# Hybrid decoder block on one core: u for z's last chunk read into idle places of the gates' tile, and two of the first merge's gates read into its first two's place

## The chip, the core and the metric

The kernel runs on one core of one Trainium2 chip. That core has a matrix engine (TensorE, PE in the profile; PEld is its load of weights), a vector engine (VectorE, DVE), a scalar engine (ScalarE, ACT), a general engine (GpSimd, POOL) and an engine that mostly issues transfers (SyncE, SP; its queue is SPq in the profile). Transfers between the device's memory and the core's on-chip memory run on 16 DMA engines beside them. Each engine works through its own list of instructions in order, and semaphores hold an instruction until what it needs is there.

The metric is the time of one execution on the device, in microseconds (us). The median of the timed runs counts.

## The reference

The input is 2048 tokens of 1024 channels. One decoder block is computed; the part that matters here is the mixer and its merge:

```python
h = _rmsnorm(x, norm_pre_mix[layer])
proj = jnp.einsum('bsd,de->bse', h, w_in[layer])
...
u = jax.nn.gelu(proj[..., U0:Z0])
z = jax.nn.gelu(proj[..., Z0:GA0])
gate_a = jax.nn.sigmoid(proj[..., GA0:GB0])
gate_b = jax.nn.sigmoid(proj[..., GB0:IN_WIDTH])
y_attn = _mixer_dilated_attention(q, k, v)
y_gmlp = _mixer_chunked_gmlp(u, z, ln_v_gain[layer], ln_v_bias[layer],
                             w_spatial[layer], b_spatial[layer])
merged = (gate_a * jnp.einsum('bse,ed->bsd', y_attn, w_branch_attn[layer])
          + gate_b * jnp.einsum('bse,ed->bsd', y_gmlp, w_branch_gmlp[layer]))
y = jnp.einsum('bsd,de->bse', merged, w_out[layer])
x = x + _rmsnorm(y, norm_post_mix[layer])
```

`_mixer_chunked_gmlp` normalises z, multiplies it per group of 128 channels with a 128 x 128 matrix over the tokens of a piece, adds a bias, and multiplies the result with u. A squared-ReLU MLP with norms of its own follows.

## The kernel before

All matrix products keep the accuracy of float32 by splitting each operand into a high and a low half (`split`: the high half by ACT or POOL at lines 70 and 72, the low half by DVE or POOL at line 78) and by three matmuls for each product (lines 95 to 97, or the inner loop before line 714). The tokens are worked on in four chunks of 512.

The program has these stages: norm and the products for q, k, v, u and z; the attention, with the product of the gates beside it; the merge and the product with w_out, chunk by chunk; and the MLP. The order of PE's instructions is written by hand. On the other engines a scheduler orders them by when it supposes that they become ready, so an edit at one place can move instructions of ACT, DVE, POOL and SP at others.

**Chunk 3 of z.** `z_chunk` makes four pieces of z for a chunk and leaves the rest of the chunk's work for `sz_out`. That function goes through the four groups g. For each it multiplies on PE (line 554), scales and adds the bias on DVE (line 561, into a tile `sb`), reads u for this group from memory (line 558, into a tile `ur`), multiplies (line 564, on DVE for chunk 3 and in place in `sb`) and stores the product (line 565). `sb` and `ur` have two buffers each for the chunks 2 and 3. For chunk 3, `sz_out` is called from `gates`.

**Gates.** `gates` is the last part of the input's product: the two gates and the first part of u, by a scheme of seven products (`PHASES`) in place of eight. PE's line is 714. Its weights come in pieces (`piece`, line 631: tiles `gr` and `ga`, each split on ACT, DVE or POOL to `spots`). Sums and copies of the products lie in the tiles `gx`, `gz` and `ga` (lines 733 and 735 are the copies by ACT). `gz` holds eight places of 512 columns, `zs[0]` to `zs[7]`; of these the first are filled first, and the later ones lie idle at the start. Results go to memory (line 728). Beside the products of the gates runs the attention's work, unit by unit: scores (lines 894 and 895), a maximum on DVE (lines 908 and 912), exponentials on ACT (line 918), a transpose and the product with v.

**The first merge.** `merge(c, ...)` is called for the chunks 2, 3, 0 and 1 in this order. It goes through eight column tiles dt. For each it fills two banks on PE: `b0` from attention with 6 matmuls, and `b1` from the gMLP with 12. It multiplies each with its gate on DVE (line 1196, for which ACT has put the gate through a sigmoid, line 1179), adds the two (line 1198) and splits the sum to the tile `mg` (ACT line 70, DVE line 78). A gate's name is (chunk, dt, branch); below it is (dt, branch), (5,0) for the first branch's gate of dt 5. A bank comes free for a later dt when DVE has read it.

The first merge (chunk 2) starts with gates read by `early_gates`: the gates of dt 0 to 2 lie in the three tiles `gates0` to `gates2`, which stand in the places of later tiles (`xr`, `gpost`, `gmlp`), and the next ones in a pool of three buffers for branch 0 and two for branch 1 (`load_gate`, line 1170). From dt 3 on the loop loads the gates (dt + 2, 1) and (dt + 3, 0). Beside this merge `spatial_out` does the rest of the gMLP for the chunks 0 and 1 (`sz_out` again) and splits the weights of w_out (`split_wo`: loads `woraw` on POOL's queue at line 1135, halves `wo`). Then `out_block` computes the product with w_out for 128 tokens at a time: it reads the input `xr` (line 1220), which lies in the place of `gates0` and so must wait until that tile is free, and uses it at line 1244. The weights of norms `gpost` and `gmlp` follow to the places of `gates1` and `gates2`. The loads of the next merge's `yt` (line 91) and gates follow on SP.

Of the kernel before, what the change touches and what calls it, by code (L numbers as in the profile page):

```python
# [8 lines left out]
F32 = mybir.dt.float32  # L9
# [7 lines left out]
P = 128  # L17
S = 2048
D = 1024
# [22 lines left out]
def block_kernel(ctx, tc, a, out):  # L42
    nc = tc.nc
    pe, act, dve, pool, sp = nc.tensor, nc.scalar, nc.vector, nc.gpsimd, nc.sync
# [95 lines left out]
    u_d = dtile([4, P, S], "ud")  # L140
    gate_d = dtile([16, P, S], "gated")
    att_d = [dtile([S, 264], f"att{g}") for g in range(3)]
    ya_d = dtile([2, P, S], "yad")
    yg_d = dtile([4, P, S], "ygd")
# [216 lines left out]
    with ExitStack() as e1a:  # L361
# [118 lines left out]
        for half in range(2):  # L480
# [19 lines left out]
            for n, (g, which) in enumerate(qk):  # L500
                w = nxt
# [44 lines left out]

    sgu = {}

    def sz_out(zp, zt, c):
        wsp, bsp, lngb = sgu[c // 2]  # L550
        for g in range(4):
            p = psum_aux(f"sz_{c}{g}")
            for i in range(4):
                pe.matmul(p[:, i * P:(i + 1) * P], zt[:, i, g * P:(g + 1) * P], wsp[:, g, :],
                          start=True, stop=True)
            t = zp.tile([P, 512], F32, name=f"sb_{c}{g}", tag="sz", bufs=2 if c > 1 else 5)
            ut = zp.tile([P, 512], F32, name=f"ur_{c}{g}", tag="ur", bufs=2 if c > 1 else 4)
            sp.dma_start(ut, u_d[g, :, c * 512:(c + 1) * 512])
            bb = bsp[:, g, :]
            bb = bass.AP(tensor=bb.tensor, offset=bb.offset, ap=[list(bb.ap[0]), [0, 4], [1, P]])  # L560
            dve.scalar_tensor_tensor(t.rearrange("p (c i) -> p c i", i=P),
                                     p.rearrange("p (c i) -> p c i", i=P), lngb[:, 0, g:g + 1], bb,
                                     op0=OP.mult, op1=OP.add)
            (dve if c == 3 or c < 2 and g % 2 else pool).tensor_mul(t, t, ut)
            sp.dma_start(yg_d[g, :, c * 512:(c + 1) * 512], t)

    def z_chunk(zp, ws, c):
        zt = zp.tile([P, 4, 512], F32, name=f"z_{c}", tag="z", bufs=2)
# [19 lines left out]
    loaded, late, zps = {}, [], {}  # L588
# [77 lines left out]
    def gates():  # L666
# [2 lines left out]
        slots = [None, hp.tile([P, 2, 2, 4, 512], F32R, name="opB", tag="hT", bufs=2)]  # L669
        zs = wp.tile([P, 8, 512], F32, name="gz", tag="w", bufs=3)  # L670
        zs = [zs[:, n] for n in range(8)]
        xs = [st.tile([P, 512], F32, name=f"gx{n}", tag="ev", bufs=3) for n in range(3)]
        g_["b"].update({(1, 1): hT[2][:, :, :4], (1, 2): hT[2][:, :, 4:]})
        phases = [(half, ops) for half in (1, 0) for ops in PHASES]
        starts, t = {}, 0
# [3 lines left out]
        for t, (half, i, n) in enumerate(seq):  # L679
# [16 lines left out]
            elif todo and (t - t0) % 3 == 1 and t > t0 + 1:  # L696
                w, k = todo.pop(0)
# [13 lines left out]
            p, w, h = bank[n], g_["w"].pop(t), g_["b"][half, i]  # L711
            for k in range(4):
                for m, (l, r) in enumerate(((0, 0), (0, 1), (1, 0))):
                    pe.matmul(p, w[:, l, k], h[:, r, k], start=i in (1, 6, 5, 4) and not k and not m,  # L714
                              stop=k == 3 and m == 2, skip_group_check=True)
                if (t, k) == (3, 2) and late:
                    sz_out(*late.pop(0))
                yield
            if t == 3:
                a = [ga.tile([P, 512], F32, name=f"ga{n_}", tag=f"ga{n_}", bufs=1) for n_ in range(12)]  # L720
# [35 lines left out]
            if i in (2, 5, 3, 4):  # L756
                c, dst = 2 * half + o[2], gate_d if n < 8 else u_d
# [391 lines left out]
    gates = {}  # L1149
# [15 lines left out]
    def load_gate(c, dt, wch):  # L1165
        if dt < KT and (c, dt, wch) not in gates:
            d = chunks.index(c) * KT + dt
            pl, tag = (gtp, f"gt{wch}") if c == 2 or d % (5 - 2 * wch) < 3 - wch else (gxp[0], f"gx{wch}")
            gt = pl.tile([P, 512], F32, name=f"g{wch}_{c}{dt}", tag=tag, bufs=3 - wch if pl is gtp else 2 - wch)
            sp.dma_start(gt, gate_d[wch * 8 + dt, :, c * 512:(c + 1) * 512])  # L1170
            gates[c, dt, wch] = gt
# [10 lines left out]
    def merge(c, yt, between, each=None):  # L1182
        cs = slice(c * 512, (c + 1) * 512)
        mg = []
        for dt in range(KT):
            dsl = slice(dt * P, (dt + 1) * P)
            if dt % 4 == 0:
                mg.append(mgp[dt // 4].tile([P, 2, 4, 512], F32R, name=f"mg{c}{dt}", tag="mg"))
            parts = []
            for wch, ks in ((0, range(0, 2)), (1, range(2, 6))):  # L1190
                open_gate(c, dt, wch)
                gt = gates.pop((c, dt, wch))
                p = psum_mm(f"b{wch}_{c}{dt}")
                for k in ks:
                    mm3(p, wb[k][:, 0, dsl], wb[k][:, 1, dsl], yt[k][:, 0, :], yt[k][:, 1, :], k == ks[0], k == ks[-1])
                dve.tensor_mul(gt, gt, p)
                parts.append(gt)
            dve.tensor_add(parts[0], parts[0], parts[1])
            split(mg[-1][:, 0, dt % 4, :], mg[-1][:, 1, dt % 4, :], parts[0])
            if c != 2:  # L1200
                load_gate(c, dt + 5, 0)
                load_gate(c, dt + 3, 1)
            elif dt > 2:
                load_gate(c, dt + 2, 1)
                load_gate(c, dt + 3, 0)
            if dt < KT - 1:
                for wch in range(2):
                    open_gate(c, dt + 1, wch)
            if each:
                each(dt)  # L1210
            if dt in between:
                between[dt]()
        return mg
# [879 lines left out]
```

## Time and profile before

| what | us |
|---|---|
| timed runs, median of 3 | 2657.37 |
| timed runs, lowest and highest | 2655.06 and 2658.37 |
| the profiled execution's own time | 2654.54 |
| span of the profiled execution | 2652.4 |
| PE busy | 2619.2 |
| DVE busy | 1662.9 |
| POOL busy | 1209.3 |
| ACT busy | 1093.2 |

The mean clock that was granted to PE in the profiled execution is 0.995 of full speed.

A profile's rows are read so. A row of a timeline gives the start of an instruction in the span, its duration (or that of a group of equal ones in a row, with their number behind x), the engine, the line of the program, the operation, the tile it writes and the tiles it reads; in brackets stands for how long the engine was idle ahead of it and what it then waited for. A matmul's row is longer than its share of PE's time, since the next one starts before it ends: matmuls of 512 columns start some 0.23 us apart at full clock, though each row has 0.39. A row "A <- B: total, times, longest" of the view of waits sums the idle time of an engine by what ended it. A row of the view of windows starts with a stretch of time and its length and then has each engine's busy time, PE's granted clock, the share of the DMA engines' time and the GB/s moved.

### The profile page before, as it was taken

The page shows a single profiled execution, that of the slowest core. Times are in us where ns is not written, and L with a number is a line of the kernel's source. Part 1 is how long each engine was busy: PE and PEld are TensorE (multiplying, and loading weights), DVE is VectorE, ACT ScalarE, POOL GpSimd, SP SyncE. Part 2 cuts the span into 40 slices and gives each one's busy share as a digit, 9 for nine tenths or more (in the row PEclk, how much of TensorE's full clock was granted, in tenths as well). Part 3 has the DMA queues.
Part 4 walks back from the last instruction along what each step waited for, and adds up shares of the span by engine and source line. Part 5 has one row for each costly group of instructions (what it writes and reads, how often), then busy time and mean ns, then how long its engine had stood idle before and what let it go on. Part 6 is the DMA issues. An engine that isn't in the chain of part 4 may idle for free. (4 is left out here: it accounts for less than half of the span.)

```text
span 2652.4 us, 35505 instructions
## 1 busy us (share of the span) xinstructions
PE 2619.2 (99%) x12458; PEld 2186.1 (82%) x12458; DVE 1662.9 (63%) x2795; ACT 1093.2 (41%) x2285; POOL 1209.3 (46%) x1093
## 2 busy tenths in 40 slices
PE   9999999999999999899999999999999999999998
PEld 8888888888888878688888888888888888888886
DVE  5676565534533456855677654655437888888866
ACT  5213211244455444444446555655545333323334
POOL 0363354365455555311324473233215677676645
PEclk9999999999999999899999999999999999999999
DMA  8779778888888888744656565644343221222235
GB/s 313 284 249 324 258 232 285 290 281 260 284 296 237 241 289 285 261 149 156 218 192 253 152 222 152 223 132 123 117 145 108 88 77 67 88 88 88 88 114 212
DMA packets 388996, 525.15 MB, mean 198 GB/s; under 512 B 56977, under 2 KB 242065, under 8 KB 387794
## 3 DMA queue, kind: packets, MB, share of 16 engines
q1 hardware_dynamic: 300048, 432.88, 49.7%
q0 software_dynamic: 14992, 51.65, 5.1%
q10 hardware_dynamic: 73778, 38.35, 4.8%
q8 instruction: 98, 1.61, 0.2%
q14 instruction: 80, 0.66, 0.1%
HBM read 339.62 MB, written 183.17 MB: 197 GB/s over the span
## 5 line engine op out<-in xcount | busy, mean ns | idle before, releaser
L1944 PE MATMUL ya<-T_spots,s 128*128 128x512 f32 x1176 | 289.2, 389 | 0.7 <-ACT T_spots L70 0.5
L70 ACT ACTIVATE s<-sraw 128x768 fp32r<-128x768 f32 (+1 forms) x184 | 127.2, 696 | 330.3 <-POOL sraw L1745 155.7
L1944 PEld LDWEIGHTS ya<-T_spots,s 128*128 128x128 f32 x1176 | 220.5, 188 | 47.4 <-ACT T_spots L70 0.9
L78 DVE TENSOR_TENSOR s<-sraw,s 128x512 fp32r<-128x512 f32 x172 | 184.2, 1095 | 8.5 <-ACT s L70 7.2
L1415 PE MATMUL aa<-B,A 128*128 128x512 f32 x768 | 182.3, 390 | 0.7 <-DVE A L85 0.7
L1386 POOL TENSOR_TENSOR s<-w1r 128x512 f32<-128x512 f32 x32 | 42.3, 1321 | 306.6 <-DVE S L78 250.4
L714 PE MATMUL g<-opA,spots 128*128 128x512 f32 x672 | 170.5, 398 | 1.9 <-DVE cv L746 1.9
L1415 PEld LDWEIGHTS aa<-B,A 128*128 128x128 f32 x768 | 143.8, 188 | 31.2 <-DVE A L85 1.1
L714 PE MATMUL g<-opB,spots 128*128 128x512 f32 x648 | 164.3, 397 | 0.8 <-POOL spots L78 0.8
L1944 PE MATMUL yc<-T_spots,s 128*128 128x512 f32 x624 | 159.6, 389 | 0.0
L95 PE MATMUL x<-hT_a,wq 128*128 128x512 f32 x384 | 149.7, 390 | 0.0
L96 PE MATMUL x<-hT_a,wq 128*128 128x512 f32 x384 | 149.4, 389 | 0.0
L97 PE MATMUL x<-hT_a,wq 128*128 128x512 f32 x384 | 149.4, 389 | 0.0
L714 PEld LDWEIGHTS g<-opA,spots 128*128 128x128 f32 x672 | 121.0, 188 | 23.9 <-issue 2.3
L78 POOL TENSOR_TENSOR spots<-gr,spots 128x512 fp32r<-128x512 f32 x98 | 127.5, 1305 | 22.3 <-DMA gr<-in_w_in_dram 15.3
L1944 PEld LDWEIGHTS yc<-T_spots,s 128*128 128x128 f32 x624 | 117.1, 188 | 24.3
L714 PEld LDWEIGHTS g<-opB,spots 128*128 128x128 f32 x648 | 116.7, 188 | 22.4 <-POOL spots L78 1.3
L70 ACT ACTIVATE hl<-r 128x512 fp32r<-128x512 f32 x48 | 30.4, 633 | 235.3 <-POOL r L321 89.0
L964 DVE TENSOR_REDUCE o<-po 128x256 f32<-128x512 f32 x48 | 33.2, 692 | 133.5 <-PE po L963 133.5
L1744 POOL TENSOR_TENSOR sraw<-sraw 128x256 f32<-128x256 f32 x56 | 41.8, 747 | 161.8 <-DVE s L78 158.8
L72 POOL TENSOR_SCALAR spots<-gr 128x512 fp32r<-128x512 f32 x86 | 54.8, 637 | 133.2 <-PE g L714 98.8
L78 POOL TENSOR_TENSOR T_spots<-w2r,T_spots 128x512 fp32r<-128x512 f32 x70 | 104.4, 1520 | 7.3 <-ACT T_spots L70 7.3
(427 smaller groups left out, 6994.1 us busy)
## 6 DMA issues: line engine op xcount, KB each, us to landing
w1r<-in_w_mlp_in_dram SPq DMA_DIRECT2D x64, 512.0 KB, 3.8
sraw<-sd SPq DMA_DIRECT2D x128, 256.0 KB, 3.3
qk<-hl SPq DMA_DIRECT2D x24, 1024.0 KB, 5.5
qq<-qk SPq DMA_DIRECT2D x96, 256.0 KB, 5.2
w2r<-in_w_mlp_out_dram SPq DMA_DIRECT2D x16, 1024.0 KB, 7.8
sd<-u ACTq DMA_DIRECT2D x63, 256.0 KB, 3.2
g<-gated SPq DMA_DIRECT2D x58, 256.0 KB, 5.1
gr<-sgd SPq DMA_DIRECT2D x53, 256.0 KB, 4.8
```

The lines of the kernel that those rows point to most:

```text
L70: act.activation(hi, src, AF.Copy)
L72: pool.tensor_scalar(hi, src, 1.0, 1.0, op0=OP.mult, op1=OP.mult)
L78: (pool if lo_eng == "pool" else dve).tensor_sub(lo, src, f32(hi))
L95: pe.matmul(ps, lh, rh, start=start, stop=False)
L96: pe.matmul(ps, lh, rl, start=False, stop=False)
L97: pe.matmul(ps, ll, rh, start=False, stop=stop)
L714: pe.matmul(p, w[:, l, k], h[:, r, k], start=i in (1, 6, 5, 4) and not k and not m, stop=k == 3 and m == 2, skip_group_check=True)
L964: dve.tensor_reduce(ot[:, :, j * 64:(j + 1) * 64], po.rearrange("p (b h e) -> p b e h", b=4, h=2), axis=AX.X, op=OP.add)
L1386: pool.tensor_add(s1, a21, a22)
L1415: pe.matmul(p, w[:, l, k, :], h[:, r, k, :], start=i in (1, 6, 5) and not k and not n, stop=k == 3 and n == 2, skip_group_check=True)
L1744: pool.tensor_add(a22, a21, a22)
L1944: pe.matmul(p, s[:, l], w[r], start=i in (1, 2, 5) and not m and not o, stop=m == 1 and o == 2, skip_group_check=True)
```

## The change

The change has two parts. First, `gates` reads u for chunk 3 of z by itself: after the tile `gz` is allocated, four loads bring the four groups' u into its places 4 to 7, and `sz_out` is given these places. With them it reads nothing itself, writes the product of line 564 in place over u instead of over `sb`, and stores it from there. The tiles `ur` and the store from `sb` drop out for this chunk. Second, in the merge of chunk 2, after dt 0 a tile `gates3` takes the place of `gates0`, whose two gates are used up, and gates (5,1) and (6,0) are loaded there. From dt 3 on the loop then loads (dt + 3, 1) and (dt + 4, 0), so each of these one dt further ahead. The number of loads, stores and operations of each engine stays as it was, and the matmuls and their order too.

```diff
--- before.py
+++ after.py
@@ -546,7 +546,7 @@
 
     sgu = {}
 
-    def sz_out(zp, zt, c):
+    def sz_out(zp, zt, c, places=None):
         wsp, bsp, lngb = sgu[c // 2]
         for g in range(4):
             p = psum_aux(f"sz_{c}{g}")
@@ -554,15 +554,19 @@
                 pe.matmul(p[:, i * P:(i + 1) * P], zt[:, i, g * P:(g + 1) * P], wsp[:, g, :],
                           start=True, stop=True)
             t = zp.tile([P, 512], F32, name=f"sb_{c}{g}", tag="sz", bufs=2 if c > 1 else 5)
-            ut = zp.tile([P, 512], F32, name=f"ur_{c}{g}", tag="ur", bufs=2 if c > 1 else 4)
-            sp.dma_start(ut, u_d[g, :, c * 512:(c + 1) * 512])
+            if places:
+                ut = places[g]
+            else:
+                ut = zp.tile([P, 512], F32, name=f"ur_{c}{g}", tag="ur", bufs=2 if c > 1 else 4)
+                sp.dma_start(ut, u_d[g, :, c * 512:(c + 1) * 512])
             bb = bsp[:, g, :]
             bb = bass.AP(tensor=bb.tensor, offset=bb.offset, ap=[list(bb.ap[0]), [0, 4], [1, P]])
             dve.scalar_tensor_tensor(t.rearrange("p (c i) -> p c i", i=P),
                                      p.rearrange("p (c i) -> p c i", i=P), lngb[:, 0, g:g + 1], bb,
                                      op0=OP.mult, op1=OP.add)
-            (dve if c == 3 or c < 2 and g % 2 else pool).tensor_mul(t, t, ut)
-            sp.dma_start(yg_d[g, :, c * 512:(c + 1) * 512], t)
+            r = ut if places else t
+            (dve if c == 3 or c < 2 and g % 2 else pool).tensor_mul(r, t, ut)
+            sp.dma_start(yg_d[g, :, c * 512:(c + 1) * 512], r)
 
     def z_chunk(zp, ws, c):
         zt = zp.tile([P, 4, 512], F32, name=f"z_{c}", tag="z", bufs=2)
@@ -669,6 +673,8 @@
         slots = [None, hp.tile([P, 2, 2, 4, 512], F32R, name="opB", tag="hT", bufs=2)]
         zs = wp.tile([P, 8, 512], F32, name="gz", tag="w", bufs=3)
         zs = [zs[:, n] for n in range(8)]
+        for g in range(4):
+            sp.dma_start(zs[4 + g], u_d[g, :, 3 * 512:])
         xs = [st.tile([P, 512], F32, name=f"gx{n}", tag="ev", bufs=3) for n in range(3)]
         g_["b"].update({(1, 1): hT[2][:, :, :4], (1, 2): hT[2][:, :, 4:]})
         phases = [(half, ops) for half in (1, 0) for ops in PHASES]
@@ -714,7 +720,7 @@
                     pe.matmul(p, w[:, l, k], h[:, r, k], start=i in (1, 6, 5, 4) and not k and not m,
                               stop=k == 3 and m == 2, skip_group_check=True)
                 if (t, k) == (3, 2) and late:
-                    sz_out(*late.pop(0))
+                    sz_out(*late.pop(0), zs[4:8])
                 yield
             if t == 3:
                 a = [ga.tile([P, 512], F32, name=f"ga{n_}", tag=f"ga{n_}", bufs=1) for n_ in range(12)]
@@ -1200,9 +1206,14 @@
             if c != 2:
                 load_gate(c, dt + 5, 0)
                 load_gate(c, dt + 3, 1)
+            elif not dt:
+                w = bot.tile([P, D], F32, name="gates3", tag="xr")
+                for n, key in enumerate(((c, 5, 1), (c, 6, 0))):
+                    gates[key] = w[:, n * 512:(n + 1) * 512]
+                    sp.dma_start(gates[key], gate_d[key[2] * 8 + key[1], :, c * 512:(c + 1) * 512])
             elif dt > 2:
-                load_gate(c, dt + 2, 1)
-                load_gate(c, dt + 3, 0)
+                load_gate(c, dt + 3, 1)
+                load_gate(c, dt + 4, 0)
             if dt < KT - 1:
                 for wch in range(2):
                     open_gate(c, dt + 1, wch)
```

With the new lines the numbers behind them shift by 4 to 11: line 558 becomes 561, 565 becomes 569, 631 becomes 635, 1170 becomes 1176, 1196 becomes 1202.

How the order on the engines moves is shown at three places. The first is SP's queue where `gates` starts. Here `ygd` is the gMLP's result in memory, `ud` is u in memory, sb_20 to sb_33 and ur_22 to ur_33 are the tiles of chunk and group, `opB` is an operand of the gates' product and `gr` a piece of its weights. Before:

```order
L565 DMA ygd_78<-sb_22_4335 128x512
L558 DMA ur_30_4477<-ud_72 128x512
L565 DMA ygd_78<-sb_23_4346 128x512
L731 DMA opB_4399<-tgd_86 128x1024 x3
L558 DMA ur_31_4488<-ud_72 128x512
L731 DMA opB_4399<-tgd_86 128x1024
L631 DMA gr0_4205<-in_w_in_dram 128x4x128 x2
L728 DMA gated_73<-gz_4400 128x512
L631 DMA gr1_4206<-in_w_in_dram 128x4x128 x2
L631 DMA gr0_4205<-in_w_in_dram 128x4x128 x2
L565 DMA ygd_78<-sb_30_4476 128x512
```

And with the change:

```order
L677 DMA gz_4400<-ud_72 128x512 x2
L569 DMA ygd_78<-sb_22_4335 128x512
L569 DMA ygd_78<-sb_23_4346 128x512
L677 DMA gz_4400<-ud_72 128x512 x2
L737 DMA opB_4399<-tgd_86 128x1024 x4
L635 DMA gr0_4205<-in_w_in_dram 128x4x128
L734 DMA gated_73<-gz_4400 128x512
L635 DMA gr0_4205<-in_w_in_dram 128x4x128
L635 DMA gr1_4206<-in_w_in_dram 128x4x128 x2
L635 DMA gr0_4205<-in_w_in_dram 128x4x128
L569 DMA ygd_78<-gz_4400 128x512
```

The loads of u for chunk 3 stand two by two ahead of the store of sb_22 and behind that of sb_23, instead of between the stores and the operands, and the third and fourth no longer behind the stores of the first two products.

The second place is ACT in the first merge. Tiles g0_2n and g1_2n are the gates (n,0) and (n,1) of chunk 2, mg the sums' halves, wo the weights. Before:

```order
L70 ACTIVATE mg20_10064<-gates1_10042 128x512
L70 ACTIVATE wo4_10013<-woraw4_10140 128x1024
L70 ACTIVATE wo5_10014<-woraw5_10229 128x1024
L70 ACTIVATE mg20_10064<-gates2_10043 128x512
L70 ACTIVATE mg20_10064<-g0_23_10054 128x512
L70 ACTIVATE wo2_10011<-woraw2_10223 128x1024
L1179 ACTIVATE g1_25_10287<-g1_25_10287 128x512
L70 ACTIVATE mg24_10297<-g0_24_10058 128x512
L70 ACTIVATE wo3_10012<-woraw3_10225 128x1024
L1179 ACTIVATE g0_26_10289<-g0_26_10289 128x512
L1179 ACTIVATE g1_26_10323<-g1_26_10323 128x512
```

And with the change:

```order
L1185 ACTIVATE gates3_10088<-gates3_10088 128x512
L70 ACTIVATE mg20_10060<-gates1_10038 128x512
L70 ACTIVATE wo4_10009<-woraw4_10139 128x1024
L1185 ACTIVATE gates3_10088<-gates3_10088 128x512
L70 ACTIVATE wo5_10010<-woraw5_10228 128x1024
L70 ACTIVATE mg20_10060<-gates2_10039 128x512
L70 ACTIVATE mg20_10060<-g0_23_10050 128x512
L1185 ACTIVATE g1_26_10286<-g1_26_10286 128x512
L70 ACTIVATE mg24_10296<-g0_24_10054 128x512
L70 ACTIVATE wo2_10007<-woraw2_10222 128x1024
L1185 ACTIVATE g0_27_10288<-g0_27_10288 128x512
```

The sigmoids of (5,1) and (6,0), now both in gates3, stand ahead of dt 1's and dt 2's high halves, and ahead of dt 4's high half (mg24 from g0_24) stands the sigmoid of (6,1), g1_26, where (5,1)'s stood. POOL's queue moves with it: the load of woraw5 stood between the multiplies of sb_10 and sb_12 and now stands ahead of both; on DVE the low half of wo 1 stands right behind the sum of dt 1.

The third is DVE around the product of (5,0) (g0_25), with the same names and the banks b0 and b1. Before:

```order
L1196 TENSOR_TENSOR g1_24_10060<-g1_24_10060,b1_24_10306 128x512
L1198 TENSOR_TENSOR g0_24_10058<-g0_24_10058,g1_24_10060 128x512
L78 TENSOR_TENSOR wo2_10011<-woraw2_10223,wo2_10011 128x1024
L78 TENSOR_TENSOR mg24_10297<-g0_24_10058,mg24_10297 128x512
L1196 TENSOR_TENSOR g0_25_10062<-g0_25_10062,b0_25_10331 128x512
L78 TENSOR_TENSOR wo3_10012<-woraw3_10225,wo3_10012 128x1024
L1196 TENSOR_TENSOR g1_25_10287<-g1_25_10287,b1_25_10339 128x512
```

And with the change:

```order
L1202 TENSOR_TENSOR g1_24_10056<-g1_24_10056,b1_24_10305 128x512
L1204 TENSOR_TENSOR g0_24_10054<-g0_24_10054,g1_24_10056 128x512
L1202 TENSOR_TENSOR g0_25_10058<-g0_25_10058,b0_25_10328 128x512
L78 TENSOR_TENSOR mg24_10296<-g0_24_10054,mg24_10296 128x512
L78 TENSOR_TENSOR wo2_10007<-woraw2_10222,wo2_10007 128x1024
L1202 TENSOR_TENSOR gates3_10088<-gates3_10088,b1_25_10336 128x512
L78 TENSOR_TENSOR wo3_10008<-woraw3_10224,wo3_10008 128x1024
```

The product of (5,0) stood behind the low half of dt 4 (mg24) and now stands ahead of it; the sum of dt 4 is ahead of both as before.

## Prediction

> **What bounds the kernel now.** I read the page first, for which engine sets the time, and then the waits of that engine alone, since only they can be shortened by a change that leaves its instructions as they are.
>
> ```profile
> span 2652.4 us, 35505 instructions
> PE 2619.2 (99%) x12458; PEld 2186.1 (82%) x12458; DVE 1662.9 (63%) x2795; ACT 1093.2 (41%) x2285; POOL 1209.3 (46%) x1093
> PE b L95 <- DVE g L1196: 3.5, 2, 2.5
> PE g L714 <- ACT ga L733: 1.7, 1, 1.7
> ```
>
> The matrix engine is busy for 99% of the span, so a change that leaves all its 12458 matmuls and their order alone can win only what PE loses in waits and at a low clock. The last two rows (what PE waited for: us in total, times, longest) hold the two longest waits of the places that this change touches. The chain of work that ended last covers only the end of the program, far from both places, and gives nothing for them. Every microsecond PE gains there moves all that follows.
>
> **Part A: u for z's chunk 3.** The timelines of PE, of VectorE (DVE), of ScalarE (ACT) and of SyncE's queue (SP) over the start of gates show how the two PE waits come about.
>
> ```profile
> 539.93 3.02 PE L714 MATMUL g<-hT_a,spots 128*128 128x512 f32 x12 [0.29 <-ACT gx L733]
> 552.76 0.28 PE L895 MATMUL s<-kp,qq 128*128 128x256 f32 x1
> 554.69 0.96 PE L714 MATMUL g<-hT_a,spots 128*128 128x512 f32 x3 [1.66 <-ACT ga L733]
> ...
> 530.88 0.75 DVE L561 SCALAR_TENSOR_TENSOR sb<-sz,lngb,bsp 128x512 f32<-128x512 f32 x1 [0.64 <-issue]
> 533.80 0.69 DVE L564 TENSOR_TENSOR sb<-sb,ur 128x512 f32<-128x512 f32 x1 [0.78 <-DMA ur<-ud]
> 542.99 0.75 DVE L561 SCALAR_TENSOR_TENSOR sb<-sz,lngb,bsp 128x512 f32<-128x512 f32 x1 [8.49 <-PE g L714]
> 545.59 0.87 DVE L564 TENSOR_TENSOR sb<-sb,ur 128x512 f32<-128x512 f32 x1 [1.85 <-DMA ur<-ud]
> 547.15 1.71 DVE L564 TENSOR_TENSOR sb<-sb,ur 128x512 f32<-128x512 f32 x1
> ...
> 550.38 0.21 ACT L915 ACTIVATE nm<-o 128x4 f32<-128x4 f32 x1 [5.86 <-DVE o L908]
> 554.07 0.57 ACT L733 ACTIVATE ga<-g 128x512 f32<-128x512 f32 x1
> ...
> 531.62 7.86 SPq L631 DMA_DIRECT2D gr<-in_w_in_dram  x4
> 539.57 0.46 SPq L565 DMA_DIRECT2D ygd<-sb  x1
> 540.08 0.42 SPq L558 DMA_DIRECT2D ur<-ud  x1
> ```
>
> PE waits 1.66 us for the copy `ga` on ACT (554.07). ACT gets there late because the row at 550.38 waited 5.86 us for the attention's maximum on DVE, and DVE stood from 534.5 to 543.0 in front of the third group's line 561. The row blames a matmul, but what it needs is a free `sb`: the store at 539.57 is what empties it, and that store is queued on SP behind four weight loads (531.62, 7.86 us) that are waiting for their own places. After that DVE waits 1.85 us more for `ur`, which is loaded only at 540.08.
>
> After the change the four pieces of u have places of their own, so their loads stand ahead of the stores of the chunk before (as the order of SP in the section on the change shows), and line 561 of groups 2 and 3 needs no store, but only the `sb` that the multiply of group 0 or 1 has read. From the first row of group 0 (530.9) eight DVE operations of 0.69 to 0.87 us follow back to back and end at 530.9 + 8 x 0.7 = 536.5 instead of 548.9, if u is there by then. I put the two late loads at 524, behind the last store of the chunk before; a load of u took 545.59 - 540.08 = 5.5 us at the most in these rows, so they land by 529.5, ahead of need. The attention's chain behind it then ends some 8 us earlier at most; the chain up to the `ga` copy is limited by what stands ahead of it by then, PE's own scores and ACT's queue, and I put the copy at 549 to 550 instead of 554. PE asks for it at 553.0. The margin is 3 us, so the whole wait goes. From 552.76 to 554.69 are 1.93 us where PE's pitch is 0.12: **1.8 us**.
>
> The small wait (0.29 us) hangs on weights `gr`:
>
> ```profile
> 538.00 1.40 ACT L70 ACTIVATE spots<-gr 128x512 fp32r<-128x512 f32 x2 [0.80 <-DMA gr<-in_w_in_dram]
> 539.30 0.58 ACT L733 ACTIVATE gx<-g 128x512 f32<-128x512 f32 x1
> ```
>
> ACT copies `gx` at 539.30 only behind splits of `gr`, and the last two of these (538.00) wait for loads that SP began to issue at 531.62. Two loads of `ur` (some 0.45 us each to issue on SP) leave the queue between the stores and these loads, so `gr` starts about 0.7 us sooner; that covers 0.29, and with the matmul pipeline's restart (0.45 us from the last matmul's end to a full pitch) I book **0.45 us**. If the two moved loads only pushed `gr` back it would be a loss instead (rival 3). Part A: 1.8 + 0.45 = **2.25 us**. Elsewhere it adds nothing: four loads, four stores, eight DVE operations before and after.
>
> [...]
>
> **Part B: two gates in the first merge.** PE's rows, and the granted clock of stretches of it (columns: PE, PEld, DVE, ACT and POOL busy, PEclk, DMA share, GB/s):
>
> ```profile
> 1110.56 0.39 PE L97 MATMUL b<-yt,wb 128*128 128x512 f32 x1
> 1113.41 0.50 PE L95 MATMUL b<-yt,wb 128*128 128x512 f32 x1 [2.46 <-DVE g L1196]
> 1119.35 0.40 PE L95 MATMUL o<-wo,mg 128*128 128x512 f32 x1
> ...
> 1100.00:1110.00 10.00, 10.00 (x46) 8.21 (x45) 7.35 (x10) 3.28 (x4) 0.02 (x1) 1.00 1.00 371
> 1116.00:1118.00 2.00, 2.00 (x6) 1.54 (x6) 0.49 (x2) 1.81 (x3) 0.00 (x0) 0.50 0.87 268
> ```
>
> PE waits 2.46 us, and then the granted clock falls, to 0.50 from 1116 to 1118. From 1110.56 to 1119.35 are 8.79 us with 19 matmul starts (the last product of (6,1)'s bank, 18 of dt 7), which at the pitch of the rows around (0.23) take 4.4: the place costs 8.8 - 4.4 = **4.4 us**. What it waits for:
>
> ```profile
> 1112.07 0.69 DVE L78 TENSOR_TENSOR mg<-g,mg 128x512 fp32r<-128x512 f32 x1 [2.39 <-ACT mg L70]
> 1112.67 0.68 DVE L1196 TENSOR_TENSOR g<-g,b 128x512 f32<-128x512 f32 x1
> 1110.88 0.63 ACT L1179 ACTIVATE g<-g 128x512 f32<-128x512 f32 x1 [4.14 <-DMA g<-gated]
> 1111.42 0.61 ACT L70 ACTIVATE mg<-g 128x512 fp32r<-128x512 f32 x1
> 1104.91 11.73 SPq L1170 DMA_DIRECT2D g<-gated  x5
> 1108.46 1.22 DVE L78 TENSOR_TENSOR wo<-woraw,wo 128x1024 fp32r<-128x1024 f32 x1
> 1082.60 0.68 DVE L78 TENSOR_TENSOR mg<-gates,mg 128x512 fp32r<-128x512 f32 x1
> ```
>
> PE's bank of dt 7 comes free when DVE has multiplied gate (5,0), at 1112.67. That stands on DVE behind the low half of dt 4 (1112.07), which waits for the high half on ACT (1111.42), which stands behind the sigmoid of gate (5,1) (1110.88), whose load was issued at 1104.91 and took 5.96 us while the transfers were at a share of 1.00. DVE itself was ready for (5,0) at 1109.7, after 1108.46's row.
>
> After the change (5,1) and (6,0) are loaded when dt 0's low half (1082.60) is done, at 1083.3, so their sigmoids are long over. Moreover DVE has (5,0) ahead of the low half of dt 4. The wait for (5,0) goes; what is late next is gate (6,1), whose load now takes the place in the queue that (5,1)'s had, and whose sigmoid now stands on ACT ahead of dt 4's high half.
>
> ```profile
> 1095.29 0.60 POOL L1135 DMA_DIRECT2D woraw<-in_w_out_dram  x1
> 1101.97 1.06 ACT L70 ACTIVATE wo<-woraw 128x1024 fp32r<-128x1024 f32 x1 [7.20 <-DMA woraw<-in_w_out_dram]
> 1089.17 0.67 DVE L1198 TENSOR_TENSOR gates<-gates 128x512 f32<-128x512 f32 x1
> 1104.19 0.68 DVE L1198 TENSOR_TENSOR g<-g,g 128x512 f32<-128x512 f32 x1
> 1098.53 0.75 SPq L1220 DMA_DIRECT2D xr<-in_x_dram  x1
> 1137.00 1.28 DVE L1244 SCALAR_TENSOR_TENSOR xr<-y,r_post,xr 128x1024 f32<-128x1024 f32 x1
> g<-gated SPq DMA_DIRECT2D x58, 256.0 KB, 5.1
> ```
>
> Its place comes free at the sum of dt 3 (1104.19 to 1104.87), which stands behind `wo` 5's split (1101.97), whose load POOL issued at 1095.29, behind a multiply that waited for u. In the new order POOL issues it ahead of that multiply, as soon as DVE has done `wo` 1's low half behind the sum of dt 1 (1089.17): 1089.8 + 1.2 = 1091. The split then runs at 1098, and the sum of dt 3 ends at about 1103.3, an estimate: 1.6 us sooner, since PE's own matmuls of dt 4 stand ahead of it by then. The load of (6,1) is issued there. PE first needs what hangs on it at 1112.2 (1110.56 + 0.23 for the end of dt 6, and six matmuls of the other bank): the bank of (7,1), freed by the multiply of (5,1). Behind the landing stand the sigmoid (0.63), dt 4's high half (0.61), `wo` 2's high half on ACT (1.06) and low half on DVE (1.22), and the multiply (0.68), 4.2 us in all. So the load may take until 1112.2 - 4.2 = 1108.0, or 4.7 us, without PE waiting. The nearest row from above is (5,1)'s own 5.96 us, the page's median of all such loads 5.1 (its last column: us to landing). What argues for less: the 512 KB load `xr` of 1098.53 no longer stands ahead of it, and `woraw` 5 is under way 4 us sooner; 768 KB less at the 371 GB/s of 1100 to 1110 is worth some 2 us. I take 4 us, near 5.96 - 2, with 3.5 and 5.96 as the ends. So **4.4 us** go; at 5.96 a wait of 1.3 us would come in their place, short as those that no low clock follows, and B would be 3.1.
>
> The load `xr` is now issued at about 1117.8, when dt 6's low half has freed its place, and two loads of `yt` with the next merge's gates stand behind it on SP. DVE uses `xr` first at 1137.00 (line 1244), 19 us later, three times the longest load worked out here: nothing. The next merge starts later still, beyond 1137: nothing.
>
> On the clock: the rows show a wait of 2.46 us followed by the granted clock 0.50, while PE's waits of 1.66 us (554.69) and less were not. [...]
>
> **The sum.** The profiled execution took 2654.54 us (span 2652.4); 2.25 + 4.4 = 6.65 less is 2647.9. The median of the three timed runs is 2657.37 (2655.06 to 2658.37), so the same gain gives **2650.7**.
>
> **Rivals.** (1) Only part A: gate (6,1), in (5,1)'s place, holds up ACT and DVE as (5,1) did. From 7.2 us after issue (1103.3 + 7.2 + 4.2 = 1114.7) PE waits 2.5 us for the other bank, and the low clock follows as before: B is nothing. For it: the share of 1.00 from 1100 to 1110. Against: what leaves the queue. 2657.37 - 2.25 = 2655.1.
>
> (2) Slower: waits of 1 us or more that follow each other in the first merge hold the clock down. The stretch after 1064 shows the price:
>
> ```profile
> 1067.14 0.80 PE L96 MATMUL b<-yt,wb 128*128 128x512 f32 x1 [1.69 <-POOL yt L78]
> 1072.00:1076.00 4.00, 3.12 (x8) 1.83 (x7) 3.93 (x5) 2.70 (x4) 4.00 (x5) 0.50 0.93 304
> ```
>
> There the clock stays at 0.50 until 1080, where each matmul costs 0.43 instead of 0.23. If (6,1) lands after 1112, 8.7 us after issue, PE would wait about 4 us and then run 31 matmuls 0.2 us slower: 4 + 6.2 = 10.2 against 4.4 before, +5.8, less A's 2.25: 2661. That is half as long again as (5,1) took.
>
> (3) A partly lost: u's loads delay `gr`. Two more loads of 256 KB ahead, each about 0.7 us (256 KB at the 371 GB/s of the busiest stretch), put the `gx` copy 1.4 us later: the wait of 0.29 becomes 1.6. A falls from 2.25 to about 0.5, the gain to 4.9: 2652.5.
>
> (4) The low clock isn't the wait's doing: B is 2.6, the gain 4.85, 2652.5.
>
> (5) The change doesn't do what it says, since an unseen wait takes each place: 2657.4.
>
> **How the numbers follow.** Chances: forecast 0.60, (1) 0.16, (3) 0.10, (4) 0.06, (5) 0.04, (2) 0.04. The range 2646.5 to 2657.5 takes in the forecast with the runs' own spread (4 us below) and all rivals but the slower one. 0.2%, about what a measurement of this kernel can tell from no change, is 5.3 us, and the forecast's 6.65 lies only 1.3 beyond: it falls inside 0.2% in about one case of five, and (3) and (4) beyond it in two of five. Faster by over 0.2%: 0.6 x 0.8 + 0.16 x 0.4 = 0.54, with a little of (1) 0.55; slower 0.03; the rest 0.42.
>
> **What would show it.** A right: DVE's four multiplies of chunk 3 end before 538, and PE's rows have no wait for `ga` or `gx` between 535 and 556; a longer wait on ACT's `gx` is rival 3. B right: no PE wait above 1 us near 1110, clock 1.00 there, sigmoid of (6,1) before 1108. A sigmoid after that with a wait on the second bank is rival 1; a wait gone with the clock at 0.50 is rival 4. The prediction is wrong if PE's waits elsewhere grow: above all the `yt` waits after 1064, which stay as they are here.

## The result, and the profile after

The changed kernel takes 2648.76 us (median of 20 runs, 2646.07 to 2660.86) against 2657.09 us before (20 runs, 2652.32 to 2661.44). The ratio is 0.9974 with a 95% interval of 0.9967 to 0.9982: 6.9 us less, between 4.8 and 8.8. (The ratio rests on all the runs; the two medians alone lie 8.3 us apart, the two means 6.6.) Its profiled execution took 2647.32 us with a span of 2645.3, 7.1 less than the 2652.4 of before. The forecast was 6.65 less, by 2.25 in part A and 4.4 in part B.

**Part A.** Rows of the changed kernel's timelines where gates begins, PE, DVE, ACT and SP's queue in this order:

```profile
530.47 9.13 PE L720 MATMUL g<-hT_a,spots 128*128 128x512 f32 x39
549.52 0.86 PE L720 MATMUL g<-hT_a,spots 128*128 128x512 f32 x3
...
530.84 1.28 DVE L568 TENSOR_TENSOR gz<-sb,gz 128x512 f32<-128x512 f32 x2
532.82 0.69 DVE L568 TENSOR_TENSOR gz<-sb,gz 128x512 f32<-128x512 f32 x1
...
541.47 0.21 ACT L921 ACTIVATE nm<-o 128x4 f32<-128x4 f32 x1 [0.29 <-DVE o L914]
545.08 0.58 ACT L739 ACTIVATE ga<-g 128x512 f32<-128x512 f32 x1
...
521.52 0.93 SPq L677 DMA_DIRECT2D gz<-ud  x2
526.28 8.78 SPq L635 DMA_DIRECT2D gr<-in_w_in_dram  x4
535.15 0.46 SPq L569 DMA_DIRECT2D ygd<-gz  x1
```

The 27 and 12 matmuls that stood apart by 0.29 us are one row of 39, and the three matmuls that waited 1.66 us have no bracket. DVE is done with the four products at 533.5 and idle after it; ACT no longer waits 5.86 us for the maximum but 0.29, and the copy `ga` starts at 545.08, 4.4 us before PE asks for it at 549.52. The store of the first product still leaves only at 535.15, behind the weights' loads, but nothing waits for it now.

**Part B.** The first merge, from the timelines and the view of windows of the changed kernel:

```profile
1107.57 0.50 PE L95 MATMUL b<-yt,wb 128*128 128x512 f32 x1 [0.72 <-DVE gates L1202]
1106.00:1108.00 2.00, 1.28 (x6) 0.76 (x5) 2.00 (x3) 1.65 (x3) 0.53 (x1) 1.00 0.28 95
1108.00:1110.00 2.00, 2.00 (x10) 1.60 (x9) 1.90 (x4) 0.63 (x1) 0.53 (x1) 1.00 0.82 232
...
1097.79 3.38 SPq L1176 DMA_DIRECT2D g<-gated  x3
1103.56 0.63 ACT L1185 ACTIVATE g<-g 128x512 f32<-128x512 f32 x1 [5.13 <-DMA g<-gated]
1104.10 0.61 ACT L70 ACTIVATE mg<-g 128x512 fp32r<-128x512 f32 x1
1106.84 0.68 DVE L1202 TENSOR_TENSOR gates<-gates,b 128x512 f32<-128x512 f32 x1
```

The wait of 2.46 us for the product of (5,0) is gone and the granted clock stays at 1.00. A shorter one, 0.72 us, stands 12 matmuls ahead of the end of dt 7 now: PE waits for (7,1)'s bank, which the product of (5,1) at 1106.84 frees. The rows show the chain that the prediction named: the load of (6,1) was issued at 1097.79, its sigmoid ran 5.77 us later, dt 4's high half stood behind it (1104.10), and DVE behind that.

**By place.** PE runs the same 12458 matmuls in the same order in all kernels here, so the time from the start of one numbered matmul to that of another can be compared from profile to profile. Counted from 0, part A's place is from matmul 2560 to 2700 and part B's from 5600 to 5760 (the last two dt and the first product with w_out):

| profiled execution | part A's place | part B's place | matmuls 1100 to 1300 | span |
|---|---|---|---|---|
| before | 28.94 | 41.16 | 35.00 | 2652.4 |
| before, second profile | 29.01 | 42.54 | 34.25 | 2651.2 |
| part A alone | 26.41 | 43.66 | 41.57 | 2658.7 |
| part B alone | 29.39 | 38.05 | 35.85 | 2650.8 |
| reads early only | 26.42 | 37.67 | 36.16 | 2646.4 |
| products' place only | 27.84 | 38.11 | 40.23 | 2653.8 |
| changed | 26.42 | 37.66 | 34.24 | 2645.3 |
| changed, second profile | 26.43 | 37.92 | 40.31 | 2653.3 |

The rows between are experiments below. Part A's place is worth 2.5 us (28.94 and 29.01 against 26.42 and 26.43). Part B's is 42.45 us in the mean of the three profiles without part B's edit and 37.88 in the five of this table with it: 4.6 us, between 3.1 and 6.0 by pairs. The sum, 7.1, fits the ratio. The fourth column is far ahead of the change, at about 240 us, and differs by up to 7.3 us from one execution to the next.

### The profile page after: what moved, and what is told of

Same layout as the page of the kernel before. It is cut to its first block, busy times and chain, and to the rows that moved or that the text cites. A ratio compares the mean times of both kernels' runs of the same rounds, so it can differ in the third digit from the quotient of the medians.

```text
span 2645.3 us, 35504 instructions
## 1 busy us (share of the span) xinstructions
PE 2614.4 (99%) x12458; PEld 2183.1 (83%) x12458; DVE 1668.4 (63%) x2795; ACT 1094.1 (41%) x2285; POOL 1210.3 (46%) x1093
```

## The experiments

**Each part alone.** The first kernel keeps part A and loads the first merge's gates as before; the second has only part B. The first one's edit of the changed kernel:

```diff
-            elif not dt:
-                w = bot.tile([P, D], F32, name="gates3", tag="xr")
...
             elif dt > 2:
-                load_gate(c, dt + 3, 1)
-                load_gate(c, dt + 4, 0)
+                load_gate(c, dt + 2, 1)
+                load_gate(c, dt + 3, 0)
```

> The change's part A alone (u for chunk 3 in the gates' tile; the first merge loads its gates as before). My theory, that the two parts gain apart from each other: the waits of PE for the copies ga (1.66) and gx (0.29) are gone, 2.4 us as in the changed kernel's profile; the wait near 1110 (2.46 us, released by the product of gate (5,0)) is there again, followed by a clock of 0.50; about 2.4 us faster than the kernel before, 2654.7 on its median of 2657.1, which a timing can hardly tell from no change. Rival, that part A moves the later merge too through its order of instructions: the wait near 1110 is shorter than 2 us. Rival on the clock, that its fall is a matter of when the wait falls and not of how long it is: a wait of 2 to 3 us there with the clock at 1.00.

Measured: 2653.67 us, ratio 0.9986 (0.9975 to 0.9997) to before. Its place A is 26.41 us, as in the changed kernel. In the first merge:

```profile
1117.24 0.50 PE L95 MATMUL b<-yt,wb 128*128 128x512 f32 x1 [2.23 <-DVE g L1202]
1128.44 0.50 PE L95 MATMUL o<-wo,mg 128*128 128x512 f32 x1 [2.37 <-ACT mg L70]
...
1118.00:1120.00 2.00, 1.92 (x8) 1.24 (x7) 2.00 (x4) 0.83 (x2) 0.53 (x1) 1.00 0.41 98
1130.00:1132.00 2.00, 2.00 (x6) 1.52 (x6) 2.00 (x4) 2.00 (x5) 0.00 (x0) 0.50 1.07 404
```

The wait for (5,0) is there with 2.23 us, so part A doesn't touch it, and the rival of that falls. But the clock stayed at 1.00 behind it (1118 to 1120): the second rival's sign. A second wait, 2.37 us, which the first profile of before does not have, comes 11 us later at the first matmuls of the product with w_out, and behind that one the clock is at 0.50. So the place costs 43.66 us here against 41.16.

The second one's edit is the other half of the diff, shown in the section on the change.

> The change's part B alone (two gates in the place of the first merge's first two; u for chunk 3 read and stored as before). My theory: PE waits for ga 1.6 to 1.7 us and for gx 0.3 as in the kernel before; near 1110 a wait of 0.5 to 1.3 us, released by the product of gate (5,1), with the clock at 1.00, in place of 2.46 us; 3.5 us less than before by the profile, 2653.6 on the median of 2657.1. Rival, that the load of (6,1) decides: with it landing under 4.7 us after issue there is no wait at all and 4.4 us go; over 7 us the wait is over 2.3 us and nothing is gained.

Measured: 2652.40 us, ratio 0.9988 (0.9977 to 1.0000). Its rows for both places:

```profile
539.20 3.03 PE L714 MATMUL g<-hT_a,spots 128*128 128x512 f32 x12 [0.88 <-ACT gx L733]
553.83 0.96 PE L714 MATMUL g<-hT_a,spots 128*128 128x512 f32 x3 [1.50 <-ACT ga L733]
1114.30 0.50 PE L95 MATMUL b<-yt,wb 128*128 128x512 f32 x1 [0.21 <-DVE gates L1196]
...
1105.23 3.38 SPq L1170 DMA_DIRECT2D g<-gated  x3
1110.29 0.63 ACT L1179 ACTIVATE g<-g 128x512 f32<-128x512 f32 x1 [4.42 <-DMA g<-gated]
```

The waits of part A's place are back, 0.88 and 1.50 us; part B's wait is 0.21 us, under the 0.5 to 1.3 that were expected, and (6,1)'s sigmoid ran 5.06 us after the load's issue. The two parts gain apart from each other. The intervals of both ratios are too wide to say more than that each is between nothing and 6.6 us; the sizes are in the profiles.

**The halves of part A.** Part A gives u early reads, and the products a place that no store has to empty. One kernel keeps only the first, one only the second:

```diff
-            r = ut if places else t
+            r = t
```

> The changed kernel, but the product of u and the gating term is written over sb and stored from there as before; only the reads of u are early. So groups 2 and 3 wait for the stores of groups 0 and 1 again. If the stores queued behind the weights' loads are enough to hold PE (each half of the edit is needed): the wait for ga is back at 1 us or more. If either half is enough: DVE's third group starts 6 to 10 us after the second instead of at once, its last product ends 8 to 10 us later than in the changed kernel (533.5 there), and the copy ga still comes before PE asks for it, no wait over 0.3 us; the spare 4.4 us of the changed kernel (545.1 against 549.5) shrink to under 2.5.

```diff
-            if places:
-                ut = places[g]
-            else:
-                ut = zp.tile([P, 512], F32, name=f"ur_{c}{g}", tag="ur", bufs=2 if c > 1 else 4)
-                sp.dma_start(ut, u_d[g, :, c * 512:(c + 1) * 512])
+            ut = zp.tile([P, 512], F32, name=f"ur_{c}{g}", tag="ur", bufs=2 if c > 1 else 4)
+            sp.dma_start(ut, u_d[g, :, c * 512:(c + 1) * 512])
...
-            r = ut if places else t
+            r = places[g] if places else t
...
-        for g in range(4):
-            sp.dma_start(zs[4 + g], u_d[g, :, 3 * 512:])
```

> The changed kernel, but u is read through the two ur buffers at the place of the kernel before; only the products go to the gates' tile. So line 561 waits for no store, but the reads of groups 2 and 3 stand in the queue behind the weights' loads and the first stores. If each half is needed: the wait for ga is back at 1 us or more. If either half is enough: the products of groups 2 and 3 wait for u and end 8 to 10 us later than in the changed kernel, and PE waits under 0.5 us for ga.

Rows of the first (early reads, products stored from `sb`), DVE, ACT and PE:

```profile
540.27 0.75 DVE L564 SCALAR_TENSOR_TENSOR sb<-sz,lngb,bsp 128x512 f32<-128x512 f32 x1 [6.66 <-DMA ygd<-sb]
550.89 0.57 ACT L739 ACTIVATE ga<-g 128x512 f32<-128x512 f32 x1
552.14 0.86 PE L720 MATMUL g<-hT_a,spots 128*128 128x512 f32 x3
```

And of the second (reads through `ur`, products in the gates' tile), DVE and PE:

```profile
550.00 2.68 DVE L565 TENSOR_TENSOR gz<-sb,ur 128x512 f32<-128x512 f32 x2 [9.35 <-DMA ur<-ud]
545.17 3.02 PE L715 MATMUL g<-hT_a,spots 128*128 128x512 f32 x12 [0.64 <-ACT gx L734]
558.50 0.96 PE L715 MATMUL g<-hT_a,spots 128*128 128x512 f32 x3 [0.23 <-ACT ga L734]
```

In the first, DVE waits 6.66 us, and here the row names the store itself (`ygd<-sb`) where the row of before named a matmul; yet the copy `ga` starts 1.25 us before PE asks, and PE doesn't wait. In the second DVE waits 9.35 us for u, and PE 0.23 us for `ga`. So either half takes nearly all of the 1.66 us away; together they make the spare time of 4.4 us. The 0.29 us for `gx` go with the early reads alone: 0.64 us are there where `ur` is still read in between.

**The same kernels once more.** Each of the two kernels, unchanged, was profiled a second time.

> The kernel before, unchanged, for a second profile. If the waits of the two places belong to the kernel: ga 1.5 to 1.8 us, gx 0.2 to 0.9, the wait for (5,0) 2.2 to 2.7 us. If what differs elsewhere between profiles (the wait for vt near 240 us, 0.0 to 4.6 in the runs so far; those for hT_b near 1020, 0 to 3.7) belongs to the execution and not to the kernel, these differ here from the first profile of the same kernel by up to 4 us. The low clock behind the wait for (5,0) may be there or not.

> The changed kernel, unchanged, for a second profile. If part A's gain belongs to the kernel: no wait for ga or gx. If the load of (6,1) is what decides the rest of part B: the wait before (7,1) is 0 to 1 us and follows the landing of that load by 3.3 us or a little more, with the clock at 1.00.

Before, second profile: 0.39 and 1.63 us of waits in part A's place, and in part B's

```profile
1109.79 0.50 PE L95 MATMUL b<-yt,wb 128*128 128x512 f32 x1 [1.75 <-DVE g L1196]
1120.26 0.50 PE L95 MATMUL o<-wo,mg 128*128 128x512 f32 x1 [1.63 <-ACT mg L70]
1110.00:1112.00 2.00, 1.93 (x8) 1.27 (x8) 2.00 (x4) 0.39 (x1) 0.53 (x1) 1.00 0.49 148
1122.00:1124.00 2.00, 2.00 (x6) 1.58 (x5) 2.00 (x5) 2.00 (x5) 0.00 (x0) 0.50 1.08 411
```

The wait for (5,0) is 1.75 us, under the expected 2.2, with the clock at 1.00 behind it; again a second wait follows, and the low clock behind that. So this second wait belongs to the kernel before as well. Changed kernel, second profile: none of the three waits, and

```profile
1106.75 3.38 SPq L1176 DMA_DIRECT2D g<-gated  x3
1111.28 0.63 ACT L1185 ACTIVATE g<-g 128x512 f32<-128x512 f32 x1 [3.89 <-DMA g<-gated]
241.58 0.79 PE L95 MATMUL va<-wv,hT_a 128*128 128x512 f32 x1 [3.23 <-DVE vt L357]
```

Here (6,1) took 4.53 us and PE didn't wait. But the whole span is 2653.3 against 2651.2 of the second profile of before, since PE waited 3.23 us near 240 us, followed by a low clock, where the changed kernel's first profile has no wait at all. With one profile of each, the pair would have told the opposite of the timing.

**One gate more read early.** If the late landing of (6,1) makes what is left of the wait, an early read of it takes that away:

```diff
-            elif not dt:
-                w = bot.tile([P, D], F32, name="gates3", tag="xr")
-                for n, key in enumerate(((c, 5, 1), (c, 6, 0))):
+            elif dt < 2:
+                w = bot.tile([P, D], F32, name=f"gates{3 + dt}", tag=("xr", "gpost")[dt])
+                for n, key in enumerate((((c, 5, 1), (c, 6, 0)), ((c, 6, 1),))[dt]):
```

> The changed kernel, with gate (6,1) too read early: into the place of the gates of dt 1, where the norm's weights go later (so that load moves behind the sum of dt 6). On ACT dt 4's high half then stands ahead of every sigmoid that waits for a late load. If the changed kernel's wait of 0.72 us (with its restart 0.9 us) before (7,1)'s first matmul is the late landing of (6,1), it is gone: no PE wait over 0.2 us from 1085 to 1112, 0.9 us less, 2647.9 on the changed kernel's median of 2648.8; the norm's weights land at 1120 or before and are needed at 1127. Rival, that DVE itself is behind there and the landing only shows in front of it: the wait stays at 0.5 us or more. Rival, that the load moved costs more than this: a new wait of PE from 1125 to 1140 of over 1 us.

Measured: 2651.00 us, ratio 0.9983 (0.9973 to 0.9992); not better than the changed kernel's 0.9974, nor to be told from it.

```profile
1113.58 0.47 PE L95 MATMUL o<-wo,mg 128*128 128x512 f32 x1 [1.38 <-DVE gates L1202]
1112.75 1.28 DVE L1202 TENSOR_TENSOR gates<-gates,b 128x512 f32<-128x512 f32 x2
1109.27 1.23 DVE L78 TENSOR_TENSOR wo<-woraw,wo 128x1024 fp32r<-128x1024 f32 x1 [1.47 <-ACT wo L70]
1107.65 0.63 ACT L1185 ACTIVATE g<-g 128x512 f32<-128x512 f32 x1 [1.17 <-DMA g<-gated]
1102.19 1.71 SPq L1176 DMA_DIRECT2D g<-gated  x2
```

The wait before (7,1) is gone, as expected, and another of 1.38 us stands at the first matmul of the product with w_out, a place that no theory had named. It is the same chain one gate on: the last loads now begin at 1102.19, the first of their sigmoids runs at 1107.65, the split of `wo` stands behind it on ACT and its low half on DVE ahead of the products that free the banks. Place B takes 39.12 us, 1.5 more than in the changed kernel.

**The clock behind a wait.** The kernel before had shown 0.50 behind 2.46 us, and part A alone 1.00 behind 2.23. Two kernels make the wait before (7,1) longer by one or two operations of DVE that leave the bank as it is:

```diff
+                if (c, dt, wch) == (2, 5, 1):
+                    for _ in range(1):
+                        dve.tensor_scalar(p, p, 1.0, 1.0, op0=OP.mult, op1=OP.mult)
                 dve.tensor_mul(gt, gt, p)
```

> The changed kernel with one more operation of DVE on the bank of (5,1) (times one in place, about 0.7 us) ahead of its product, behind which the low half of wo 3 also comes first, so that PE's wait before (7,1) grows from 0.72 us by about 1.9, to 2.6. If a wait of this length brings the low clock by itself: granted clock 0.50 within 2 us after it, and matmuls 0.43 us apart for some 3 us, which costs 1.5 us beside the wait. If only a longer wait does it or where the wait falls decides: the clock may stay at 1.00, as it did behind the 2.23 us of the run with part A alone; one run of each length can only tell that this is possible.

> As the run before, with two such operations: PE's wait grows to about 4.0 us. Over any length after which the clock was seen low here (2.37 and 2.46 us): granted clock 0.50 behind the wait, for some 3 us or longer, in every theory but the one that the clock doesn't follow a wait at all.

Rows with one operation (the first two) and with two, PE and the view of windows:

```profile
1113.23 0.50 PE L95 MATMUL b<-yt,wb 128*128 128x512 f32 x1 [1.77 <-DVE gates L1205]
1116.00:1118.00 2.00, 2.00 (x7) 1.57 (x6) 0.08 (x1) 1.17 (x2) 0.00 (x0) 0.55 0.91 347
...
1115.57 0.79 PE L95 MATMUL b<-yt,wb 128*128 128x512 f32 x1 [2.42 <-DVE gates L1205]
1116.00:1118.00 2.00, 2.00 (x6) 1.52 (x6) 1.92 (x4) 0.00 (x0) 0.00 (x0) 0.50 1.01 362
```

The waits came out shorter than expected, 1.77 and 2.42 us. One reason is that the load of (6,1) landed sooner than in the run that the 0.72 us are from: its sigmoid ran 4.43 and 5.19 us after the issue against 5.77. The other is that the second operation was priced too high: the product of (5,1) started 3.28 us behind that sigmoid in the changed kernel, 5.02 with one operation and 5.61 with two. The clock fell behind both waits, also behind the shorter one. Place B takes 39.96 and 40.48 us, 2.3 and 2.8 more than in the changed kernel, for 1.05 and 1.70 us more of waiting; the rest, a little over 1 us, is about what the low clock costs here.

## Why the prediction was right, by its steps

**Part A: 2.25 forecast, 2.5 measured.** The terms were 1.8 us for `ga` and 0.45 for `gx`. From the profile of before to that of the changed kernel the gap between the two executions grows by 1.92 us at `ga` (matmuls 2676 and 2677) and by 0.58 at `gx` (matmul 2612 and the six behind it). The mechanism held: DVE finished at 533.5 and ACT's copy came ahead of need. The spare time was put at 3 us and is 4.4.

The prediction laid the wait on the stores queued behind the weights' loads and took the late reads for a part of 1.85 us beside it. The halves showed these to be two limits, each of which nearly hides the other: take away either, and PE's wait falls to 0.23 us or none.

**Rival 3 (the reads hold up the weights)** fell: in each profile with the early reads, PE has no wait for `gx`. The last two reads were issued at 521.52, the weights' loads from 524.69 on. What the reads may have cost these loads doesn't show in PE's waits.

**Part B: 4.4 forecast, 3.5 in the first pair of profiles, 4.6 in the mean.** Three steps have to be kept apart.

The first, that the wait for (5,0) goes, held in all five profiles with the edit.

The second, the landing of (6,1), is the term that was mis-sized: 4 us were taken, and until its sigmoid it took 4.45 to 5.77. But the limit that was worked out, 4.7 us from issue to landing, held to within 0.4 us. From the issue of the load to its sigmoid, and PE's wait before (7,1):

| profiled execution | issue to sigmoid | wait |
|---|---|---|
| reads early only | 4.45 | none |
| changed, second profile | 4.53 | none |
| products' place only | 4.93 | none |
| part B alone | 5.06 | 0.21 |
| changed | 5.77 | 0.72 |

From 5.06 to 5.77 the wait grows by 0.51 for 0.71 us. The forecast's own figure for 5.96 us, a wait of 1.3 with part B at 3.1, fits the first pair's 0.72 and 3.5 as well. Rival 1 needed 7.2 us; no run came near.

The third step was the clock: that the wait of 2.46 us brings a low clock, and waits of 1.66 and less do not. The first pair of profiles shows what was booked for it: of the 3.5 us, 1.74 are the shorter wait, and the other 1.8 are the 4.4 forecast less the 2.6 of rival 4 (from 1110.56 to 1113.41 less one pitch of 0.23). As a rule it falls: of the three profiles with the old merge the clock fell behind the wait for (5,0) in one only, the first profile of before, where 2.19 us of it lay in one stretch of the clock's grid; with 1.81 us (part A alone) and 1.75 (before, second profile) in one stretch it stayed at 1.00 (last section). In these two a second wait came, 1.63 and 2.37 us, with the low clock behind that one. The cost that the first profile showed by wait and clock was there in all three (41.16 to 43.66 us), if not always by that wait; the forecast named only one of its forms. That the mean came so near to 4.4 is thus in part luck: a second wait, which the forecast didn't have, took the place of the low clock that it had.

**Rival 4 (the low clock has nothing to do with the wait)** falls with the two kernels with a longer wait, in which nothing but the wait was added ahead of (7,1) and the granted clock from 1116 to 1118 was 0.55 and 0.50 where the changed kernel's was 1.00 behind its 0.72 us, and with the count over all traces in the last section. **Rival 2 (slower)** needed (6,1) 8.7 us after issue and did not come. **Rival 5 (an unseen wait takes each place)** falls with the interval of the ratio, though one did take the place in the kernel with one more gate read early.

**Elsewhere** the two first profiles differ too: the changed one is 2.8 us ahead before part A's place begins (matmul 2560), falls back by 1.7 us and comes up again between the parts, and loses 1.8 us behind part B's place. These leave 1.1 us of the 7.1. In the second pair the rest of the program differs by 9.3 us the other way. The prediction had left it at nothing. The two profiles of each kernel can't tell, but the timing fits: 6.9 us, between 4.8 and 8.8, against the 7.1 of the two places. The later load of `xr`, also booked at nothing, cost nothing in the first pair: the gap stays at 8.9 us from matmul 5760 to 6000.

## What to carry to other kernels

A chain that ends in an engine's wait can have two limits of nearly the same length, here a store that empties a buffer and a load behind it in one queue; ask of each by itself what it would leave. When a late load is moved ahead, name the next one that takes its place in the queue and work out by when it must land: that limit held where the guess of its landing did not. And compare a change of a few us place by place, between the same two instructions of each profile; by whole spans, one pair of profiles here had the wrong sign. When a wait of PE is priced, its low clock is a second term that came in some executions here and not in others: 0.50 behind 2.46 us in the first profile of before, 1.00 behind 1.75 us at the same place in the second.

## What the hardware showed that was not expected

In these traces the low clock is no matter of a wait's length alone, but of how much of it falls into one stretch of a fixed grid. The traces keep the times at which the granted clock changes. In each of the 11 traces of this study all these times lie on a grid of 3.413 us, to within 5 ns, and each low clock, but those at the program's start and end, lasts one, two, three or four whole stretches of it. In the first profile of before the granted clock is 0.50 for 3.413 us from 18.96, for 13.653 from 1066.85 and for 3.413 from 1114.63; in that of the changed kernel for 3.413 us from 978.95 and for 6.827 from 1064.29. The grid doesn't lie the same in every execution: counted from the start of the span, the first record of the clock comes at 5.30 us in the first of these two profiles, at 6.15 in the second, and at 4.8 to 6.7 over all 11.

Some 8400 stretches at full clock, in all stages of the program, can be sorted by how long PE was idle in them: behind all 25 with 1.85 us or more the next stretch is at half clock, behind none with less than 1.54 us, and between these behind 13 of 26. The same two profiles have 1531 of these stretches: the next one is at half clock behind the five with 1.89, 1.92, 2.15, 2.19 and 2.54 us, and behind none of the others, the longest of which have 1.66 and 1.56. Behind a stretch that is at half clock already, less idle time is followed by another one at half clock: 0.58, 0.75 and 0.88 us were in the first profile of before and 1.29 in that of the changed kernel, where 0.49 was not. These are the stretches after 1064, in which the short waits hold the clock down.

So the wait for (5,0) brought the low clock in the first profile of before, where 2.19 of its 2.46 us lay in one stretch, and not with part A alone, where its 2.23 us were split into 1.81 and 0.42, nor in the second profile of before, with its 1.75 us all in one. In the kernel with one operation more, a wait of 3.19 us near 240 us, split into 1.84 and 1.35, was not followed by it, and the one of 1.77 us before (7,1), all in one stretch, was. The idle times come from ends of matmuls that the profile models; what decides between 1.54 and 1.85 us stays open.

The spread of executions has one main place. The wait for `vt` near 240 us was nothing in the changed kernel's first profile, 3.23 us in its second and 4.6 in that of part A alone, and with the low clock behind it this place took 34.24 to 41.57 us. That is as much as the whole change. Without this place and the two places of the change, the eight spans of the table lie within 3.3 us of each other. Why this wait varies stays open.
